# Three-pass projections and query-key products in f16 parts instead of float32r, in an encoder block

## The chip, the cores and the metric

One core of a Trainium2 chip runs the whole kernel. The metric is the time of an execution on the device in microseconds, as the median of several runs. A profile of one further execution comes with it. Engines are named as in the profile: PE does matmuls (PEld is its weight load), DVE, ACT and POOL work element by element on 128 partitions, and SP only issues DMAs here. Each engine runs its own instructions in order, and waits at an instruction whose input isn't there yet.

## The reference: what is computed

One layer of an encoder block on 1024 positions with 1024 features, in float32. Cut to what matters:

```python
h = x @ w_in                                   # (1024, 1024) @ (1024, 3328)
q_a, k_a, v_a, z_a, q_b, k_b, v_b, z_b = split(h)
# group a: 8 heads of 64; grid of 16 x 64 positions, window of 8 x 16 positions, bias per head
s = q_a . k_a * 64 ** -0.5 + rel_bias          # softmax over the 128 keys of the window
# group b: 8 query heads on 2 key heads, rotary positions, |i - j| <= 128, one sink logit per head
s = rotary(q_b) . rotary(k_b) * 64 ** -0.5     # softmax over the band and the sink
mixed = concat(y_a * silu(z_a), y_b * silu(z_b))
x = layer_norm(2 ** 0.25 * x + mixed @ w_out)
```

## The kernel before

**Split operands.** PE gets float32 accuracy from products of parts. An operand is split into a high part (a copy that rounds) and a low part (the rest), and each product is made of three matmuls: high with high, high with low, low with high. In this kernel the parts of x, of the input and output weights, of the queries and keys are float32r (32 bits wide); those of v and of the softmax weights are f16, with powers of two as scales, which for v are found on chip from its column maxima.

**First stage, v.** x arrives transposed in 16 tiles `xT[half, k]` of 128x512, k being one of 8 blocks of features and half one of two halves of the positions. `load_x` loads a tile into one of four `xr` buffers, ACT copies its high part, and DVE subtracts. v (640 columns) needs all of x: for the first half of the positions eight PSUM banks are filled side by side while x and the v weights arrive; then for the second half eight groups of 24 matmuls follow, one bank after the other. `v_out` (L369) copies a bank to SBUF on ACT and takes running maxima on DVE. This stage stands in a `manual_schedule` section (L377): every engine gets the instructions of that section in the order in which they are written. The rest up to the steps is ordered by the compiler.

**Projections.** The other 21 blocks of 128 columns of `w_in` are projected in the order `ORDER`: zb0, z0, zb1, kb, qb0, z1 ahead of the steps, and then 15 inside them. `project(name)` (L280) makes 2 halves x 8 k x 3 parts = 48 matmuls of 512 columns at L292. A weight block comes in two tiles m (256 KB each): `w_load` (L136) loads a tile, `w_split` (L142) makes the high part on ACT (L150) and the low part on POOL (L154). `evac` (L242) takes the result out of PSUM: a gate z by Silu or Tanh, a group-b query or key through `rope`, and queries and keys by `split_q` and `split_k` into stacks (`qs`, `ks`) that hold the high part on one half of the partitions and the low one on the other; POOL copies the key parts to the other half (L217).

**V scaling.** After zb0 the maxima of v are transposed on PE, turned into powers of two, and v is scaled, split, written to HBM and copied there into windows (`vd`, `vwin`), from which group a gathers.

**Steps.** There are 128 units, 64 of group b and then 64 of group a, one per step: 128 queries of one head against 256 to 384 keys. The section is again one of written order. In step i PE makes the two query-key matmuls of unit i (`stage_qk`, L533 and L534), DVE adds the bias and takes the minimum (L540), ACT does the exponential (L556). One step later `stage_tr` splits the weights in f16 (ACT L566, DVE L567) and SP transposes them by a DMA. Every four steps `stage_pv` (L595) multiplies four units with v, and every eight the outputs are transposed and multiplied with the gates. Between these `pump_to` puts projection matmuls, and at the end the first output matmuls, as a filling whose pace is given by `FILL_AT` (project number against step). `enq` puts splits and loads into queues per engine, from which each step takes one or two (`pop`). `stage_load` loads a bias tile four steps ahead (`LD`).

**Output.** `wo_split` splits 16 output weight tiles, eight of them in the steps at `WO_AT`, loaded at `WO_LD`; `m_queue` splits the gated outputs of group b at `M_AT`. `final` (L722) does the rest and the layer norm.

**Memory.** Pools of tiles with a fixed number of buffers: `big` (32 of 128x512 float32r) holds the parts of x and later those of the output weights; `wp` the weight tiles; `zp` the gates; `kq` the stacks, which are also used for gated outputs.

Of the kernel before, what the change touches and what calls it, by code (L numbers as in the profile page):

```python
# [23 lines left out]
PSCALE = 2.0 ** 14  # L24
LTT, LPP, BP, BH, BR, ND, NA, NX, F1 = 1, 5, 2, 7, 3, 1, 1, 6, 0.2
# [6 lines left out]
ZTAG = {"z3": "zv", "zb3": "zc", "z2": "zs"}  # L32
# [3 lines left out]
WO_TAG = ("wr", "wr", "wr", "wh", "wl", "wh", "wl", "wh", "wl")  # L36
# [12 lines left out]
def hybrid_block(ctx, tc, xT, x, wt, wv, wo, bias, sink, gain, lbias, cos, sin, bmask, out):  # L49
# [4 lines left out]
    big = ctx.enter_context(tc.tile_pool(name="big", bufs=32))  # L54
# [13 lines left out]
    def half_tile(name):  # L68
        return big.tile([128, 512], F32R, tag="big", name=name)

    xh, xl = {}, {}
    for half in range(2):
        for k in range(KT):
            xh[half, k] = half_tile(f"xh{half}{k}")
            xl[half, k] = half_tile(f"xl{half}{k}")
    zt = {}

    def zslot(name, tag="z"):
        return zp.tile([128, S], F32, tag=tag, name=name, bufs=5 if tag == "z" else 1)
# [6 lines left out]
    vsch = const.tile([128, 6], F32, name="vsch")  # L86
# [7 lines left out]
    def stk(kind):  # L94
        if kind == "q":
            return tiles["kq"].tile([128, S], F32R, tag="qs", name="qs", bufs=4)
        return tiles["kq"].tile([128, S], F32R, tag="ks", name="ks", bufs=8)
# [38 lines left out]
    def w_load(m):  # L136
        if m < NH:
            raw = wp.tile([128, 4, 128], F32, tag="wr", name=f"wr{m}", bufs=3)
            nc.sync.dma_start(raw, wt[m // 2, m % 2])
            raws[m] = raw  # L140

    def w_split(m):  # L142
# [16 lines left out]
        load_ops["w", m + 3] = enq("sp", lambda: w_load(m + 3), o)  # L159
# [3 lines left out]

    def split_q(p, half, src, dep=None):
        sl = slice(512 * half, 512 * half + 512)
        grid = not isinstance(p, str)
        ops = []

        def aps(j):
            if ("q", p, j) not in stks:  # L170
                stks["q", p, j] = stk("q")
            t = stks["q", p, j]
            a, o = slice(64 * j, 64 * j + 64), slice(64 - 64 * j, 128 - 64 * j)
            if grid:
                hi, lo = (t[r, sl].rearrange("p (b r c) -> p r b c", b=4, r=8) for r in (a, o))
                return hi, lo, src[a].rearrange("p (r b c) -> p r b c", b=4, r=8)
            return t[a, sl], t[o, sl], src[a]

        def hi(j):
            h, l, v = aps(j)  # L180
            nc.scalar.copy(h, v)

        def lo(j):
            h, l, v = aps(j)
            nc.vector.tensor_sub(l, v, h.bitcast(F32))

        prio = 0 if dep is None else 1
        for j in range(2):
            o = enq("act", lambda j=j: hi(j), dep, prio=prio)
            ops.append(enq("dve", lambda j=j: lo(j), o, prio=prio))  # L190
# [3 lines left out]
    def split_k(p, half, src, dep=None):  # L194
        sl = slice(512 * half, 512 * half + 512)
        ops, dup = [], []

        def aps(j):
            if ("kh", p, j) not in stks:
                stks["kh", p, j] = stk("kh")  # L200
                stks["kl", p, j] = stk("kl")
            return (stks["kh", p, j], stks["kl", p, j],
                    slice(64 * j, 64 * j + 64), slice(64 - 64 * j, 128 - 64 * j))

        def hi(j):
            h, l, a, o = aps(j)
            nc.scalar.activation(h[a, sl], src[a], AF.Copy, scale=0.125)  # L207

        def lo(j):
            h, l, a, o = aps(j)  # L210
            nc.vector.scalar_tensor_tensor(l[a, sl], src[a], 0.125, h[a, sl].bitcast(F32),
                                           op0=ALU.mult, op1=ALU.subtract)

        def dup_(j, w):
            h, l, a, o = aps(j)
            t = (h, l)[w]
            nc.gpsimd.tensor_copy(t[o, sl], t[a, sl])  # L217

        prio = 0 if dep is None else 1
        for j in range(2):  # L220
            o1 = enq("act", lambda j=j: hi(j), dep, prio=prio)
            o2 = enq("dve", lambda j=j: lo(j), o1, prio=prio)
            ops.append(o2)
            dup.append(enq("pool", lambda j=j: dup_(j, 0), o1))
            dup.append(enq("pool", lambda j=j: dup_(j, 1), o2))
# [3 lines left out]
    def rope(ps, half):  # L229
# [5 lines left out]
        o1 = enq("act", lambda: nc.scalar.copy(raw, ps), prio=0)  # L235
# [6 lines left out]
    def evac(name, half, ps):  # L242
# [17 lines left out]
        if name in ORDER[:3]:  # L260
            nc.scalar.activation(zt[e][:, sl], ps, AF.Silu)
            return []
        o = enq("act", lambda: nc.scalar.activation(zt[e][:, sl], ps, AF.Tanh, scale=0.5), prio=0)
# [5 lines left out]
    def z_col(e):  # L269
        c = e if e < 4 else 4 + (e - 4) // 2  # L270
        return (vsc if e in (4, 0, 5) else vsch)[:, c:c + 1]
# [8 lines left out]
    def project(name):  # L280
        n = ORDER.index(name)
        w_split(2 * n + 2)
        for half in range(2):
            ps = new_group()
            for k in range(KT):
# [5 lines left out]
                for i, (a, b) in enumerate(((h, xh), (h, xl), (l, xh))):  # L291
# [674 lines left out]
```

## Time and profile before

| | us |
|---|---|
| median of 3 runs (lowest, highest) | 483.23 (482.37, 483.33) |
| the profiled execution | 481.19 |
| its span, first to last instruction | 479.4 |
| v stage: first matmul of v to last | 3.8 to 61.9 |
| projections ahead of the steps | 61.8 to about 128 |
| steps | about 124 to 397 |
| output and layer norm | to 479.4 |

The granted clock of PE is 0.996 over the span. ACT is busy for 13.72 us of the 40 between 60 and 100, and POOL for 14.61. The longest groups of the page are the three of L292 with 336 matmuls each (133.9, 132.0 and 131.6 us); a matmul's listed length (393 to 398 ns) is from its start to its modelled end and overlaps the next one's, so that paces are read from the distances of starts, or from the merged pieces of the chain.

Durations that come up later: ACT cast of a weight tile 610 ns (L150), POOL subtraction of a weight tile 1324 ns (L154), DVE subtraction for x 690 ns (L333), DMA of a weight tile 3.1 us from issue to landing (median of 42), of a bias tile 3.7 (288 KB) and 4.6 (384 KB).

### The profile page before, as it was taken

To read this page: it belongs to the slowest core of one execution; us is meant where nothing else is said; L and a number is where in the kernel's file an instruction comes from. 1 tells how busy PE (TensorE), PEld (TensorE's weight loads), DVE (VectorE), ACT (ScalarE), POOL (GpSimd) and SP (SyncE) were. 2 spreads that over 40 slices of the span, in tenths; PEclk is the share of its full clock that TensorE was granted. 3 is DMA by queue.
4 is the path that set the end of the run, shared out by engine and by line. 5 is a ranking of instruction groups with operands and counts; after the bars stand their busy time and mean duration, and the time that the engine had idled before them with its cause. 6 is when DMAs were issued, how large, how long until landed. Compare 5 with 4: busy or idle time off the path is not lost.

```text
span 479.4 us, 9121 instructions
## 1 busy us (share of the span) xinstructions
PE 466.5 (97%) x3240; PEld 400.6 (84%) x3240; DVE 325.2 (68%) x772; ACT 255.2 (53%) x601; POOL 165.5 (35%) x153
## 2 busy tenths in 40 slices
PE   8999999999999999999999999999999999999993
PEld 6999988888788888888888888888888778788883
DVE  5726505868567968888787767767767739379644
ACT  5651122352577858777777676766768737012101
POOL 0030012597236246464124225122535317125521
PEclk9999999999999999999999999999999999999998
DMA  7862001477276666567889898999999979216211
GB/s 252 260 210 86 1 0 45 132 244 243 60 110 105 163 111 128 100 143 117 176 138 222 199 189 198 229 207 212 209 190 203 208 194 398 110 42 193 97 45 64
DMA packets 132381, 74.73 MB, mean 156 GB/s; under 512 B 101104, under 2 KB 117488, under 8 KB 132080
## 3 DMA queue, kind: packets, MB, share of 16 engines
q1 hardware_dynamic: 132192, 74.00, 66.3%
q8 instruction: 25, 0.41, 0.4%
q14 instruction: 20, 0.16, 0.1%
q10 hardware_dynamic: 144, 0.15, 0.1%
HBM read 43.72 MB, written 9.96 MB: 112 GB/s over the span
## 4 chain that ended last, share of the span: by engine, by line
PE 84%; DVE 7%; DMA 3%; ACT 3%; issue 2%; SPq 0%; ACTq 0%; DVEq 0%
PE ps_pj L292 42%; PE ps_t L595 6%; PE ps_s L705 6%; PE ps_pj L705 4%; PE ps_s L362 4%; PE ps_s L533 4%; PE ps_s L534 4%; PE ps_t L705 3%; PE ps_pj L362 3%; PE ps_t L362 3%; DMA tr<-split 2%; PE ps_ot L705 2%; PE ps_ot L362 1%; PE ps_ot L615 1%; DMA xraw<-in_xT 1%
## 5 line engine op out<-in xcount | busy, mean ns | idle before, releaser
L292 PE MATMUL ps_pj<-xh,wh 128*128 128x512 f32 x336 | 133.9, 398 | 0.8 <-ACT rp_raw L235 0.5
L292 PE MATMUL ps_pj<-xl,wh 128*128 128x512 f32 x336 | 132.0, 393 | 0.0
L292 PE MATMUL ps_pj<-xh,wl 128*128 128x512 f32 x336 | 131.6, 392 | 0.0
L154 POOL TENSOR_TENSOR wl<-wr,wh 128x512 fp32r<-128x512 f32 x42 | 55.5, 1324 | 169.5 <-ACT wh L150 119.4
L556 ACT ACTIVATE ps_s<-sn,nm 128x385 f32<-128x385 f32 (+3 forms) x128 | 70.5, 551 | 52.7 <-DVE nm L540 51.3
L567 DVE SCALAR_TENSOR_TENSOR split<-ps_s,split 128x384 f16<-128x384 f32 (+2 forms) x128 | 65.6, 513 | 20.4 <-ACT split L566 19.7
L292 PEld LDWEIGHTS ps_pj<-xh,wl 128*128 128x128 f32 x336 | 63.1, 188 | 12.9
L292 PEld LDWEIGHTS ps_pj<-xh,wh 128*128 128x128 f32 x336 | 63.2, 188 | 10.9 <-DVE z L264 0.7
L292 PEld LDWEIGHTS ps_pj<-xl,wh 128*128 128x128 f32 x336 | 63.2, 188 | 9.4
L566 ACT ACTIVATE split<-ps_s 128x384 f16<-128x384 f32 (+2 forms) x128 | 58.0, 453 | 11.6 <-DMA tr<-split 9.7
L540 DVE CUSTOM_DVE_ANT_0 sn<-ps_s,bm,nsk 128x384 f32<-128x384 f32 (+1 forms) x64 | 37.2, 582 | 19.0 <-PE ps_s L534 18.2
L540 DVE CUSTOM_DVE_ANT_0 sn<-ps_s,bias 128x288 f32<-128x288 f32 (+1 forms) x64 | 32.3, 505 | 20.9 <-PE ps_s L534 19.1
L533 PE MATMUL ps_s<-ks,qs 128*128 128x384 f32 (+2 forms) x128 | 41.3, 322 | 0.1
L534 PE MATMUL ps_s<-ks,qs 128*128 128x384 f32 (+2 forms) x128 | 41.1, 321 | 0.0
L217 POOL CAST ks<-ks 64x512 fp32r<-64x512 f32 x40 | 27.2, 679 | 35.8 <-ACT ks L207 19.4
L595 PEld LDWEIGHTS <-tr 128*128 128x128 f16 (+1 forms) x1104 | 35.6, 98 | 4.0 <-DMA tr<-split 1.7
L150 ACT CAST wh<-wr 128x512 fp32r<-128x512 f32 x42 | 25.6, 610 | 10.2 <-PE ps_pj L292 8.5
L762 ACT ACTIVATE sd<-mv,eps 128x1 f32<-128x1 f32 x8 | 2.4, 295 | 52.5 <-DVE mv L760 52.5
L533 PEld LDWEIGHTS ps_s<-ks,qs 128*128 128x128 f32 x128 | 24.0, 188 | 7.0 <-DVE split L567 1.8
L534 PEld LDWEIGHTS ps_s<-ks,qs 128*128 128x128 f32 x128 | 24.0, 188 | 5.0
L556 ACT ACTIVATION_READ_ACCUMULATOR ps_s<-sn,nm 128x1 f32 x128 | 24.1, 188 | 0.0
L671 POOL TENSOR_TENSOR wol<-wor,woh 128x512 fp32r<-128x512 f32 x11 | 15.6, 1430 | 22.8 <-ACT woh L667 19.8
(191 smaller groups left out, 871.2 us busy)
## 6 DMA issues: line engine op xcount, KB each, us to landing
wr<-in_wt SPq DMA_DIRECT2D x42, 256.0 KB, 3.1
bias<-in_bias SPq DMA_DIRECT2D x16, 288.0 KB, 3.7
wor<-in_wo SPq DMA_DIRECT2D x16, 256.0 KB, 5.3
xr<-in_x SPq DMA_DIRECT2D x8, 512.0 KB, 8.0
xraw<-in_xT SPq DMA_DIRECT2D x15, 256.0 KB, 4.5
out<-xr SPq DMA_DIRECT2D x14, 256.0 KB, 2.0
bias<-in_bias SPq DMA_DIRECT2D x8, 384.0 KB, 4.6
wvraw<-in_wv SPq DMA_DIRECT2D x7, 320.0 KB, 4.0
```

What stands on the lines that cost most here:

```text
L154: nc.gpsimd.tensor_sub(l, raws.pop(m), h.bitcast(F32))
L217: nc.gpsimd.tensor_copy(t[o, sl], t[a, sl])
L292: nc.tensor.matmul(ps, a[:, k % 4, :], b[half, k], start=(k == 0 and i == 0), stop=(k == KT - 1 and i == 2))
L362: nc.tensor.matmul(ps[:, :320], lh[t // 4, k][:, ts], rh[k][:, cs], start=(k == 0 and i == 0), stop=(k == KT - 1 and i == 2))
L533: nc.tensor.matmul(ps[:, :n], q, sl[0], start=True, stop=False)
L534: nc.tensor.matmul(ps[:, :n], q, sl[1], start=False, stop=True)
L540: nc.vector.tensor_tensor_reduce(sn[:, :n], ps[:, :n], bias_t, -1.0, init, op0=ALU.add, op1=ALU.min, accum_out=nm)
L556: nc.scalar.activation(pt[:, :m], sn[:, :m], AF.Exp, bias=nm, scale=-1.0, accum_out=sm[:, k:k + 1])
L566: nc.scalar.activation(hl[:, :m, 0, :c], src, AF.Copy, scale=PSCALE)
L567: nc.vector.scalar_tensor_tensor(hl[:, :m, 1, :c], src, PSCALE, hl[:, :m, 0, :c], op0=ALU.mult, op1=ALU.subtract)
L595: nc.tensor.matmul(ps[:, HD * m:HD * m + HD], a, b_, start=(i == 0), stop=(i == len(mms) - 1))
L705: nc.tensor.matmul(ps, lh[:, ts], rh[:, cs], start=(e == EO[0] and i == 0), stop=(e == EO[-1] and i == 2))
```

## The change

Projections of q, k and z and the query-key products use f16 parts in place of float32r parts; v and the output product keep float32r. To keep the parts in range, each operand is scaled by a power of two that the kernel finds itself: one for x (`sc[:, 0]`), one for the first four weight blocks, which are `NG0` (`sc[:, 1]`), and one for the other 17 (`sc[:, 2]`).

- x keeps its float32r parts for v. Its largest absolute value per partition is taken by 16 DVE reductions (`x_max`), `chain(0)` makes the scale of it with one PE transpose; then x is loaded a second time and split in f16 (`x16_part`: high on ACT; low on DVE, or in two operations on POOL for k = 1, 3, 5).
- The weights are loaded once more for a bound of their size (`scan_load`, `scan`: ACT Abs with a running sum, 42 tiles): eight within the v stage and 34 after it; `chain(1)` and `chain(2)` make the scales. `w_split` gets a scale on ACT and a second POOL operation, a multiplication in place.
- Scales are taken out again where results leave PSUM: `inv` for the gates, `QSCALE` for queries and keys, `sg` in the operation at L540 (a pointer in place of -1.0), and `rsg`, by which POOL multiplies each bias tile.
- The queries of group a are put in window order by the projection's moving operand and not by the split.
- The running maxima of v are taken three banks at a time, behind the parts of x.
- Output weights 0 to 3 are loaded at steps 60 to 74 and split at 67 to 79 (before: loaded at 111 to 115, split at 115 to 122); `M_AT` goes from 115 to 118 for one split. Tiles get other buffers: `big` is 16 of twice the size, the stacks are f16 and closed ahead of `final`, gated outputs lie in `big` and in `final`'s own pool.

```diff
+QSCALE = 2.0 ** -23
+NG0 = 4
-M_AT = [105, 112, 115, 120]
-WO_AT = [115, 116, 117, 122, 132, 132, 133, 133]
-WO_LD = [111, 112, 113, 115, 129, 129, 130, 130, 131, 132, 132, 133, 133]
+M_AT = [105, 112, 118, 120]
+WO_AT = [67, 71, 75, 79, 132, 132, 133, 133]
+WO_LD = [60, 61, 70, 74, 129, 129, 130, 130, 131, 132, 132, 133, 133]
...
         def hi():
-            h = wp.tile([128, 4, 128], F32R, tag="wh", name=f"wh{m}")
-            l = wp.tile([128, 4, 128], F32R, tag="wl", name=f"wl{m}")
+            h = wp.tile([128, 4, 128], F16, tag="wh", name=f"wh{m}")
+            l = wp.tile([128, 4, 128], F16, tag="wl", name=f"wl{m}")
             parts[m] = (h, l)
-            nc.scalar.copy(h, raws[m])
+            nc.scalar.activation(h, raws[m], AF.Copy, scale=scale)

         def lo():
             h, l = parts[m]
-            nc.gpsimd.tensor_sub(l, raws.pop(m), h.bitcast(F32))
+            raw = raws.pop(m)
+            nc.gpsimd.tensor_scalar(raw, raw, scale, 1.0, op0=ALU.mult, op1=ALU.mult)
+            nc.gpsimd.tensor_sub(l, raw, h)
+
+        g = 1 if m < 2 * NG0 else 2
+        scale = sc[:, g:g + 1]
...
-                for i, (a, b) in enumerate(((h, xh), (h, xl), (l, xh))):
-                    nc.tensor.matmul(ps, a[:, k % 4, :], b[half, k],
+                for i, (a, b) in enumerate(((h, x16h), (h, x16l), (l, x16h))):
+                    mv = b[half, k]
+                    if name[0] == "q" and name[1] != "b":
+                        mv = mv.rearrange("p (r b c) -> p b r c", b=4, r=8)
+                    nc.tensor.matmul(ps, a[:, k % 4, :], mv,
...
+        def scan_load(m):
+            scans[m] = vp.tile([128, 512], F32, tag="xr", name="wscan", bufs=4)
+            nc.sync.dma_start(scans[m], wt[m // 2, m % 2].rearrange("p k c -> p (k c)"))
+
+        def scan(m):
+            g = 0 if m < 2 * NG0 else 1
+            i, t = m - 2 * NG0 * g, scans.pop(m)
+            nc.scalar.activation(t, t, AF.Abs, accum_out=wm[g][:, i:i + 1])
+
+        def chain(i, src, tag):
+            g = gm[:, i:i + 1]
+            nc.vector.tensor_reduce(g, src, axis=AXX, op=ALU.max)
+            ps = bank(tag)
+            nc.tensor.transpose(ps[:, :128], g.to_broadcast([128, 128]), identf)
+            nc.vector.tensor_reduce(g, ps[:, :128], axis=AXX, op=ALU.max)
...
+        def x16_part(j):
+            half, k = x2[j]
+            raw = x2raw.pop(j)
...
+            nc.scalar.activation(h, raw, AF.Copy, scale=sc[:, 0:1])
+            if k in (1, 3, 5):
+                nc.gpsimd.tensor_scalar(raw, raw, sc[:, 0:1], 1.0, op0=ALU.mult, op1=ALU.mult)
+                nc.gpsimd.tensor_sub(l, raw, h)
+            else:
+                nc.vector.scalar_tensor_tensor(l, raw, sc[:, 0:1], h, op0=ALU.mult, op1=ALU.subtract)
...
             for i in range(8):
                 v_out(banks[i], i // 2, i % 2)
+            for k in range(4, KT):
+                x_max(0, k)
+            for k in range(KT):
+                x_max(1, k)
             for i in range(8):
                 ps = bank(tags[i])
                 for k in range(KT):
                     v_mms(ps, 4 + i // 2, i % 2, k)
                 v_out(ps, 4 + i // 2, i % 2)
+                if i < 2:
+                    for m in range(4 * i, 4 * i + 4):
+                        scan(m)
+                        if i == 0:
+                            scan_load(m + 4)
+                        else:
+                            x2_load(m - 4)
+                if i == 1:
+                    chain(0, xm, "ot")
+                if 2 <= i < 6:
+                    for j in range(4 * (i - 2), 4 * (i - 2) + 4):
+                        x16_part(j)
+                        x2_load(j + 4)
+                if i == 2:
+                    for m in range(4):
+                        w_load(m)
+                if i == 3:
+                    chain(1, wm[0], "ot")
+                if i == 4:
+                    w_split(0)
+                    w_split(1)
+                if i == 5:
+                    for nm, src, tag in (("cos", cos, "zc"), ("sin", sin, "zs")):
+                        tiles[nm] = zslot(nm, tag)
+                        nc.sync.dma_start(tiles[nm], src)
+                    nc.vector.tensor_scalar_mul(nsk, sk, -1.0)
+                if i > 1:
+                    v_max(3)
...
+        for m in range(2 * NG0, 2 * NG0 + 4):
+            scan_load(m)
         pump_all(["zb0"])
+        for m in range(2 * NG0, NH):
+            scan(m)
+            if m + 4 < NH:
+                scan_load(m + 4)
...
-                st["bias"] = bt
+                bv = bt[:, :, :n]
+                op = enq("pool", lambda: nc.gpsimd.tensor_scalar(bv, bv, rsg, -1.0, op0=ALU.mult, op1=ALU.mult),
+                         prio=0)
+                st["bias"] = bt, op
...
-        nc.vector.tensor_tensor_reduce(sn[:, :n], ps[:, :n], bias_t, -1.0, init,
+        c = 0 if g == "b" else 1
+        nc.vector.tensor_tensor_reduce(sn[:, :n], ps[:, :n], bias_t, sg[:, c:c + 1], init,
                                        op0=ALU.add, op1=ALU.min, accum_out=nm)
...
-    pump_all(ORDER[1:NPRO])
+    pump_all(ORDER[1:NG0 - 1])
+    chain(2, wm[1], "ot")
...
+    pump_all(ORDER[NG0 - 1:NPRO])
```

More of the change, by code (lines that the diff above doesn't have):

```diff
@@ L234, in rope @@
         sw = tiles["ap"].tile([128, 512], F32, tag="va", name="rp_sw", bufs=5)
-        o1 = enq("act", lambda: nc.scalar.copy(raw, ps), prio=0)
+        o1 = enq("act", lambda: nc.scalar.activation(raw, ps, AF.Copy, scale=QSCALE), prio=0)
         o2 = enq("dve", lambda: nc.vector.stream_shuffle(sw, raw, SWAP), o1)
@@ L640, in hybrid_block, with m_alloc @@
     EO = (4, 5, 6, 7, 0, 1, 2, 3)
-    def m_alloc(e, pair):
-        mh[e], ml[e] = (stk(pair) for _ in range(2))
+    def m_alloc(e, pool):
+        tag, bufs = ("big", 16) if pool is big else ("m", 8)
+        mh[e], ml[e] = (pool.tile([128, S], F32R, tag=tag, name=f"m{e}", bufs=bufs) for _ in range(2))
     def m_split(e, sl, hi, lo):
```

195 lines of the change are left out of this document (116 added, 79 removed).

## The prediction

> **What bounds the kernel now.** I read the page's engine table first, then the 40 slices, the chain that ended last, and then stretches of the chain in order of time.
>
> ```profile
> PE 466.5 (97%) x3240; PEld 400.6 (84%) x3240; DVE 325.2 (68%) x772; ACT 255.2 (53%) x601; POOL 165.5 (35%) x153
> ...
> PE   8999999999999999999999999999999999999993
> ```
>
> PE works in every slice but the last, and the chain gives it 84% of the span. A busy PE isn't yet a fast one, so the next question is the distance from one matmul to the next. Three pieces of the chain, about step 32, show it:
>
> ```profile
> 187.29 1.39 PE ps_pj L292 x6
> 188.68 0.12 PE ps_s L533
> 188.80 0.11 PE ps_s L534
> ...
> 190.51 0.98 PE ps_t L595 x33
> ```
>
> Six projection matmuls of 512 columns take 1.39 us, so one costs 0.231 us; in zb0 (61.95 to 72.86, 48 of them) it is 0.227. 33 f16 matmuls of 64 columns, each with its own weights, take 0.98, or 0.0295 each. The rows of weight loads say that the two kinds load at different rates, and PE's timeline that the kernel begins with six f16 matmuls of 512 columns (start, length, then the group):
>
> ```profile
> L292 PEld LDWEIGHTS ps_pj<-xl,wh 128*128 128x128 f32 x336 | 63.2, 188 | 9.4
> ...
> L595 PEld LDWEIGHTS <-tr 128*128 128x128 f16 x816 | 26.7, 98 | 3.0 <-DMA tr<-split 1.4 <-issue 1.3
> ```
>
> ```profile
> 1.19 2.74 PE L322 MATMUL ps_ot<-warm 128*128 128x512 f16 x6 [1.19 <-DVE warm L319]
> ```
>
> DVE is the next engine: 95.6 of the 120 us from 130 to 250, ACT 87.7.
>
> **The gain on PE.** Columns stream at one rate whatever the type (projection, 512 columns, 0.227; v, 320 columns, 7.04 us for 48 or 0.1467: 0.0803 for 192 columns, or 0.418 ns a column), so a float32r matmul is 512 x 0.418 = 0.214 and 0.013 to 0.017 more. An f16 matmul of 64 columns is 0.0268 and 0.0027 more. No row has an f16 matmul of 512 columns at full clock: the six of the start stand 0.438 apart (1.19 to 3.82), twice the 0.219 that is wanted, on a clock that I take to be half. Bounds: 0.214, and 0.231 as now; I take 0.217, since the f16 row with real weights is nearest.
> - Prologue, six projections: 288 x (0.227 - 0.217) = 2.9 us, and some 0.3 of stalls: 3.2.
> - Steps, fifteen projections: 720 x (0.231 - 0.217) = 10.1. After each PV block the first float32r matmul stands 0.31 before the next one (191.33 to 191.64); with f16 weights that is 0.217, for some 30 blocks 2.4 more beyond what is counted.
> - Query-key, 256 matmuls: those of 384 columns are 0.175 (0.35 a pair, 1.74 us between two steps' fills less 1.39), for f16 0.163: 160 x 0.012 = 1.9; the 96 smaller at 0.008, 0.8.
> - Off it: between 350 and 410 PE has 57.65 of 60 us, and waits there for transposes (3.7 to 4.1 us each in the chain); what PE gains there it waits, so I take off 1.3. And L540 gets a pointer in place of an immediate. Today its b form, with one pointer operand, takes 616 ns, the a form without 555 (both 384 columns), so up to 0.06 us for each of 128 units. DVE would be at about 99 of 112 us in the stretch after 130. Bounds 0 to 7.7 (all of it on the path); I take 1.5.
>
> The steps so give 15.2 - 2.8 = 12.4 us, the prologue 3.2.
>
> **What is added ahead of zb0.** The diff puts into the second half of v (33.8 to 61.8, eight groups of 24 matmuls, 3.52 us each) a maximum of x, eight weight scans, a second load of x and its f16 split. That section keeps its written order on each engine: DVE sat idle for sk although v was copied long before.
>
> ```profile
> 39.83 0.17 DVE L402 TENSOR_SCALAR nsk<-sk 128x8 f32<-128x8 f32 x1 [9.91 <-DMA sk<-in_sink]
> 39.91 0.48 DVE L372 SCALAR_TENSOR_TENSOR vmax<-v,vmax 128x320 f32<-128x320 f32 x1
> ```
>
> So I follow the order. ACT comes to scan 0 behind the copy of group 0, at 37.8. A scan is a 128x512 cast (0.61), an accumulator read (0.19) and a little: 0.85 (0.82, a 128x512 ACTIVATE with two pointers, L796, and the read would be 1.0). Scans 0 to 3 end at 41.3, each frees an xr buffer, the loads land 2.6 us later (72.00 to 74.60 for one wr load alone; 3.1 is the median), scans 4 to 7 end at 45.2. Each frees a buffer for the second x: the first is there at 45.3, and the scale of x (three reductions, a transpose, five small DVE operations at 0.17) by 42.2. A part then costs ACT 0.70 (0.61 and a pointer) and DVE 0.69, or, for k = 1, 3, 5, POOL two operations. The subtraction is a 1.30 row. The multiplication has no like row: a 64x512 cast 0.68, the only TENSOR_SCALAR 1.075 for 256 columns, so 0.7 to 2.15; I take 1.3, as for the TENSOR_TENSOR of this width.
>
> GpSimd is the place for a rule: the Trainium skill ("GPSIMD Engine Reference", section 4.1) says that it is about half as fast as VectorE for operations with two inputs and roughly at line rate with one. By its section 3.1 one input of 512 columns would be some 0.77 us (an estimate), a pair 2.1 and not 2.6, and the stall below 7.7 and not 8.8; the 1.075 row for 256 columns speaks against it, and I stay with 2.6.
>
> Part 1 leaves POOL at 49.7, part 3 at 52.3. The SP queue is written in order, so load 7 goes out at 52.4 and lands at 55.0; ACT 55.7, DVE 56.5. Only behind this does DVE reach the reduction for the first range of the weights, and its transpose lies **on PE between groups 3 and 4**. PE ends group 3 at 48.0 and waits to 56.8: 8.8 us. Bounds: 7.6 (multiplication 0.7, twice), 10.5 (2.15, and 1.8 more in zb0), and 1.2 on top with loads of 3.1. From there groups 4 to 7 cover the rest: the last x part is ready near 75.6 and zb0 wants it at 79. Without that cover zb0 itself would wait nearly as long, since x isn't split before 71. With the transpose and its wait zb0 starts at 70.9, not 61.8: 9.1.
>
> A stall that long also costs clock:
>
> ```profile
> 470.00:479.40 9.40, 1.31 (x12) 1.10 (x10) 4.19 (x9) 1.44 (x3) 1.67 (x2) 0.80 0.15 56
> ```
>
> After PE's last matmul at 471.3 the mean grant is 0.80; a fall to half gives that if it comes 4.3 us after PE stops. At the start PE needed from 1.2 to about 4.7 for the full pace. 3.5 us at half is 1.75 lost, once. (0 if the grant holds.)
>
> The twelve maxima and the later vmax fill a DVE that had 9.9 us free; bm, sk, cos and sin wait for nothing. They cost nothing unless DVE runs past 79, where zb0 still has its own cover.
>
> **The second range.** The 34 other scans (256 KB each, on SP like the rest) reuse the four buffers, from 67.6 to 75.6 on. A turn is 2.6 + 0.85 + 0.1 for four: 0.89 each, 30 us; ACT has 29 us of scans and 13.7 of other work (its busy time from 60 to 100). So they end between 108 and 118; with 1.7 for the chain and 0.7 for ACT's part, qb0, the first that needs it, has weights between 111 and 121. PE comes to qb0 at 72.7 + 4 x 10.4 = 114.3, and its third matmul wants POOL's part, 2.6 later. I take 2.5 us (0 to 9).
>
> **In the steps** POOL gets 30 multiplications (39 us by the value above) and 24 bias scalings of 576 or 768 columns (1.4 to 1.9 by 1.3 for 512; 38 us), on 130 us busy of 355. Each bias scaling also holds POOL's queue until the load lands (3.7 to 4.6): behind it lie the weight subtractions, wanted eight steps later, and key copies; the scaled bias is wanted four steps, some 8 us, later. I cost it at nothing; one late turn in three would be 8 x 2 = 16 us, but POOL's lag shortens the wait that it follows. The four early output splits take 2.5 of ACT and 4.3 of POOL away from steps 115 to 122, where nothing waits for them; their loads go onto SP at steps 60 to 74, 0.4 us of issue each, between transposes that SP issues every 2 us. Key and query splits keep their counts and widths.
>
> **Sum.** 9.1 + 1.75 + 2.5 - 3.2 - 12.4 = -2.25, and some 0.6 that the four early output splits may save where ACT is at 8.1 of 10 (340 to 350): -3. The profiled run took 481.19 around a span of 479.4; its median beside others is 483.23, 2.0 higher. 478.2 in a like run, **480.2** as a median.
>
> **Rivals.**
> - *The prologue hides better* (0.24). Multiplication at 0.7, scans done by 108, DVE never late: 7.9 + 1.75 - 3.2 - 15.2 - 0.6 = -9.4: 474. For it: DMA lies idle from 40 to 70, 0.0 of 10 us. Against: the order on PE is written down.
> - *The second range comes late* (0.17, slower). Same place, PE ahead of qb0, one mechanism: the scan loads fall behind the copies of v into its windows. A weight load behind these took 12.3 us and not 2.6. 9.7 later: 490. It decides from 3 us on. For: both move to about 110. Against: the scans stand first in the program.
> - *DVE becomes the bound in the steps* (0.11, slower). It is at 8.8 of 10 from 210 to 220; pointer operands and a faster PE bring it past 9. Half the step gain lost, 6.2: 486.5.
> - *f16 streams no faster at 512 columns* (0.05, slower): no gain at all, 9.1 + 1.75 + 2.5 - 0.6 = +12.8: 496.
> - The change does what it says: the types are in the diff.
>
> **Numbers.** The forecast has 0.43, with 475 to 486 of its own. A run of this kernel tells about 0.2%, 1 us, from none. Faster: the hidden prologue 0.24 and 0.29 of the forecast. Slower: the three rivals, 0.33, and 0.06 of the forecast. Same: 0.08. The range, 471 to 492, leaves out the last rival, the ends of the late range and the best of the hidden one.
>
> **What would show it.** Projection matmuls 0.217 apart. A PE gap ahead of v's fifth group of 24, ended by DVE, near 8.8 us, and slow matmuls behind it; zb0 from about 72.7. A small gap before qb0. Steps with DVE near 9 of 10 and no PE gap. I am wrong in sign if the two gaps together pass 14 us, or if PE waits for DVE or a scaled bias in the steps.

## The result and the profile after

| | before | changed |
|---|---|---|
| median of 4 runs (lowest, highest) | 482.80 (481.50, 483.33) | 537.27 (534.91, 539.32) |
| span of the profiled execution | 479.4 | 533.7 |
| zb0's first matmul | 61.8 | 75.2 |
| qb1's first matmul (seventh projection) | 129.8 | 161.2 |
| projections 7 to 14 (group b's half of the steps) | 128.3 | 124.9 |
| projections 15 to 21 (group a's half) | 114.8 | 142.5 |
| from the last projection to the end | 106.5 | 105.1 |

The change costs 54 us: the ratio is 1.113 [1.107, 1.120]. 31 of them arise ahead of the steps and 28 in the second half of the steps; the first half and the output give 5 back. From the page of the changed kernel, the lines that answer to those shown of before, and the chain's shares:

```profile
PE 466.1 (87%) x3243; PEld 302.3 (57%) x3243; DVE 359.5 (67%) x823; ACT 296.5 (56%) x701; POOL 220.9 (41%) x231
...
PE   8997697796599999899997839599788999999994
...
PEclk9999699989699999999999987799799999999998
...
PE 60%; DMA 11%; issue 8%; DVE 7%; ACT 7%; POOL 6%; SPq 1%; POOLq 0%; ACTq 0%; DVEq 0%
```

PE works as long as before (466 us), though its matmuls are shorter, since some of them ran at half clock (below), and it has 55 us more of idle time: in slices 4 to 11 and 22 to 31, counted from 1, and around PE's holes the granted clock falls. The groups on the page (before the bar busy us and mean ns of one, behind it idle time and what ended it) name who ended the waits:

```profile
L296 PE MATMUL ps_pj<-xf,wl 128*128 128x512 f16 x336 | 130.2, 389 | 29.1 <-POOL wl L163 29.1
L296 PEld LDWEIGHTS <-wh 128*128 128x128 f16 x672 | 64.8, 99 | 73.5 <-issue 9.3
...
L162 POOL TENSOR_SCALAR wr<-wr,sc 128x512 f32<-128x512 f32 x42 | 34.1, 812 | 67.6 <-ACT wh L157 50.6
...
L614 POOL TENSOR_SCALAR bias<-bias,rsg 128x576 f32<-128x576 f32 (+1 forms) x24 | 19.2, 798 | 90.6 <-DMA bias<-in_bias 63.0
```

PE waited 29.1 us for low parts of weights, which POOL makes. In the profile of before the matmuls with a low part of a weight had no wait:

```profile
L292 PE MATMUL ps_pj<-xh,wl 128*128 128x512 f32 x336 | 131.6, 392 | 0.0
```

POOL is busy for 41% only. It waits itself, 63 us for bias loads (L614), and whatever is behind it in its queue waits too. The matmuls themselves are as forecast: a weight load is 99 ns (188 before), and the starts of the 1008 projection matmuls stand 0.216 us apart in the median.

### The profile page after: what moved, and what is told of

Read it like the earlier page. It is cut to its first block, busy times and chain, and to the rows that moved or that the text cites. A ratio compares the mean times of both kernels' runs of the same rounds, so it can differ in the third digit from the quotient of the medians.

```text
span 533.7 us, 9570 instructions
## 1 busy us (share of the span) xinstructions
PE 466.1 (87%) x3243; PEld 302.3 (57%) x3243; DVE 359.5 (67%) x823; ACT 296.5 (56%) x701; POOL 220.9 (41%) x231
## 4 chain that ended last, share of the span: by engine, by line
PE 60%; DMA 11%; issue 8%; DVE 7%; ACT 7%; POOL 6%; SPq 1%; POOLq 0%; ACTq 0%; DVEq 0%
PE ps_pj L296 25%; PE ps_s L828 6%; PE ps_t L702 5%; PE ps_t L828 4%; PE ps_pj L828 4%; DMA wscan<-in_wt 4%; DMA bias<-in_bias 3%; PE ps_pj L366 3%; ACT wscan L388 3%; POOL wl L163 3%; PE ps_s L639 3%; PE ps_t L366 3%; PE ps_s L640 2%; PE ps_ot L828 2%; PE ps_s L366 2%
## 5 line engine op out<-in xcount | busy, mean ns | idle before, releaser
L296 PE MATMUL ps_pj<-xf,wh 128*128 128x512 f16 x672 | 207.3, 388 | 8.9 <-ACT wh L157 5.5
L296 PE MATMUL ps_pj<-xf,wl 128*128 128x512 f16 x336 | 130.2, 389 | 29.1 <-POOL wl L163 29.1
L296 PEld LDWEIGHTS <-wh 128*128 128x128 f16 x672 | 64.8, 99 | 73.5 <-issue 9.3
L663 ACT ACTIVATE ps_s<-sn,nm 128x385 f32<-128x385 f32 (+3 forms) x128 | 70.3, 549 | 63.9 <-DVE nm L647 62.8
L296 PEld LDWEIGHTS <-wl 128*128 128x128 f16 x336 | 33.5, 100 | 72.5 <-POOL wl L163 34.2
L162 POOL TENSOR_SCALAR wr<-wr,sc 128x512 f32<-128x512 f32 x42 | 34.1, 812 | 67.6 <-ACT wh L157 50.6
L647 DVE CUSTOM_DVE_ANT_0 sn<-ps_s,bias,sg 128x288 f32<-128x288 f32 (+1 forms) x64 | 36.1, 565 | 37.5 <-PE ps_s L640 30.2
L614 POOL TENSOR_SCALAR bias<-bias,rsg 128x576 f32<-128x576 f32 (+1 forms) x24 | 19.2, 798 | 90.6 <-DMA bias<-in_bias 63.0
L163 POOL TENSOR_TENSOR wl<-wr,wh 128x512 f16<-128x512 f32 x42 | 49.7, 1185 | 3.2
L647 DVE CUSTOM_DVE_ANT_0 sn<-ps_s,bm,nsk 128x384 f32<-128x384 f32 (+1 forms) x64 | 40.8, 638 | 8.9 <-PE ps_s L640 8.3
L639 PE MATMUL ps_s<-ks,qs 128*128 128x384 f16 (+2 forms) x128 | 40.2, 314 | 6.0 <-DVE split L674 4.7
L640 PE MATMUL ps_s<-ks,qs 128*128 128x384 f16 (+2 forms) x128 | 40.2, 314 | 0.0
L157 ACT ACTIVATE wh<-wr,sc 128x512 f16<-128x512 f32 x42 | 29.4, 709 | 11.9 <-PE ps_pj L296 11.9
L828 PE MATMUL ps_s<-wo,m 128*128 128x512 f32 (+1 forms) x144 | 32.5, 374 | 0.0
```

Of the source, the lines that this page charges most:

```text
L163: nc.gpsimd.tensor_sub(l, raw, h)
L296: nc.tensor.matmul(ps, a[:, k % 4, :], mv, start=(k == 0 and i == 0), stop=(k == KT - 1 and i == 2))
L639: nc.tensor.matmul(ps[:, :n], q, sl[0], start=True, stop=False)
L640: nc.tensor.matmul(ps[:, :n], q, sl[1], start=False, stop=True)
L647: nc.vector.tensor_tensor_reduce(sn[:, :n], ps[:, :n], bias_t, sg[:, c:c + 1], init, op0=ALU.add, op1=ALU.min, accum_out=nm)
L663: nc.scalar.activation(pt[:, :m], sn[:, :m], AF.Exp, bias=nm, scale=-1.0, accum_out=sm[:, k:k + 1])
```

## The experiments

Times are medians. The expectations count projections from 0, so that group a's half is 14 to 20; it begins with q1, and not with k2 as the text of e2 has it. A wait of PE is given as the profile's idle time; the expectations give some of them up to 0.2 us longer. All runs are shown against runs of the kernel before on the same chip (481.7 to 482.2).

### Bias scaling on POOL: e2, e4, e12

e2 takes it away: group a's queries and keys get their true size where they are split, and L647 gets -1.0 again.

```diff
-                op = enq("pool", lambda: nc.gpsimd.tensor_scalar(bv, bv, rsg, -1.0, op0=ALU.mult, op1=ALU.mult),
-                         prio=0)
...
-                              src[a], dep is None)
+                              src[a], kinv[a, :] if dep is None else None)
```

> Group a's queries and keys are brought to true size in their splits, so POOL scales no bias tile and the softmax operation of group a has its immediate again; all else as in the changed kernel. Theory: the bias scaling stands on POOL's queue until its load lands, the weight subtractions lie behind it, and SP's next weight load (with the transposes behind it) waits for these; the second half of the projections in the steps costs 28 us more than before (k2 to the last projection matmul 142.5 against 114.8). Then 503 to 511, and no PE wait over 1.5 us is ended by POOL in the steps. Rival: POOL's multiplication of each weight tile and the pointer operands are the price. Then 529 or more, with the waits for POOL's weight subtraction still there.

512.82 (508.36 to 515.54): 24.5 us less than the changed kernel, and group a's half takes 116.9 instead of 142.5. The time is 1.8 above the theory's range, and far from the rival's: one slow projection is left (q2, 22.6 us), in which PE waits 2.4 us for a cast of ACT and 1.5 for a low part. e4 keeps the operation and only queues it three steps behind its load, so that POOL doesn't stand at it while the load is under way.

```diff
                 op = enq("pool", lambda: nc.gpsimd.tensor_scalar(bv, bv, rsg, -1.0, op0=ALU.mult, op1=ALU.mult),
-                         prio=0)
+                         Later(), prio=0)
```

> The changed kernel with each bias scaling put into POOL's queue three steps after its load, and not in the same step; the work is the same. If POOL's waiting for the load is the cost in the second half of the steps: 505 to 515. If it is POOL's work: 530 or more. If the scaled bias then comes too late for DVE, the time lies between, with DVE waiting for POOL at the softmax operation.

515.32 (513.43 to 516.12), 22 less and 0.3 above the range for the waiting, with the same 19.2 us of POOL work; the 2.5 us to e2 lie within the spread of the runs. So it is mainly not the work that costs, it is the place in the queue. How it passes on can be read in the timelines of the changed kernel's POOL, SP and PE (start, length, work, and in brackets the idle time before it and what ended it):

```profile
308.32 2.49 POOL L794 TENSOR_TENSOR wo<-wor,wo 128x512 fp32r<-128x512 f32 x2
318.54 0.74 POOL L614 TENSOR_SCALAR bias<-bias,rsg 128x576 f32<-128x576 f32 x1 [7.73 <-DMA bias<-in_bias]
319.26 0.69 POOL L162 TENSOR_SCALAR wr<-wr,sc 128x512 f32<-128x512 f32 x1
320.03 1.15 POOL L163 TENSOR_TENSOR wl<-wr,wh 128x512 f16<-128x512 f32 x1
```

```profile
302.06 1.21 SPq L677 DMA_TRANSPOSE tr<-split  x1
308.39 0.33 SPq L146 DMA_DIRECT2D wr<-in_wt  x1
308.82 2.87 SPq L677 DMA_TRANSPOSE tr<-split  x1
...
315.05 0.57 SPq L612 DMA_DIRECT2D bias<-in_bias  x1
```

```profile
321.24 0.61 PE L296 MATMUL ps_pj<-xf,wl 128*128 128x512 f16 x1 [4.89 <-POOL wl L163]
```

It is a ring. SP stands from 303.3 to 308.39 at a weight load whose buffer POOL frees with its subtraction (307.21 to 308.36). Behind that load lie the transposes and the next bias load, which so goes out at 315.05 only. POOL reaches that bias at 310.8, waits 7.7 us for it, and the subtraction that PE needs stands behind. The lag of one engine becomes the lag of the other. Over group a's half SP's waits for POOL's low parts add up as follows (us in total, times, longest), where the kernel before has none:

```profile
SPq L146 <- POOL wl L163: 20.4, 7, 5.0
```

e12 puts this one part into the kernel before, alone, with a factor of 1:

```diff
+                op = enq("pool", lambda: nc.gpsimd.tensor_scalar(bv, bv, one, 1.0, op0=ALU.mult, op1=ALU.mult),
+                         prio=0)
+                st["bias"] = bt, op
...
+            need(op)
```

> The kernel before with one part of the change alone: POOL multiplies each bias tile, by 1, in the operation and at the place of the changed kernel. Theory (POOL waits at the head of its queue for a bias load; weight subtractions stand behind it, and SP waits for POOL before the next weight load, with transposes behind): 12 to 25 us slower, 494 to 507, and projections 14 to 20 take 127 or more instead of 114.8. Rival (it needs POOL's doubled weight work beside it): less than 5 us slower.

496.47 (494.82 to 498.92), ratio 1.029 [1.024, 1.035]: 14.2 us, and group a's half 129.3. The same ring with nothing else of the change (SP waits 16.4 us for POOL's low parts here, and DVE 7.3 us for the scaled bias), from its groups, SP, POOL and PE:

```profile
L514 POOL TENSOR_SCALAR bias<-bias,one 128x576 f32<-128x576 f32 (+1 forms) x24 | 19.3, 803 | 88.8 <-DMA bias<-in_bias 71.9
```

```profile
322.08 1.21 SPq L576 DMA_TRANSPOSE tr<-split  x1
327.36 0.34 SPq L141 DMA_DIRECT2D wr<-in_wt  x1
```

```profile
326.05 1.29 POOL L156 TENSOR_TENSOR wl<-wr,wh 128x512 fp32r<-128x512 f32 x1
333.08 0.91 POOL L514 TENSOR_SCALAR bias<-bias,one 128x768 f32<-128x768 f32 x1 [5.75 <-DMA bias<-in_bias]
333.95 1.27 POOL L156 TENSOR_TENSOR wl<-wr,wh 128x512 fp32r<-128x512 f32 x1
```

```profile
335.28 0.50 PE L294 MATMUL ps_pj<-xh,wl 128*128 128x512 f32 x1 [2.21 <-POOL wl L156]
```

### Scans, search and multiplications: e1, e3, e5

e1 sets the scales by memset (x 2^12, weights 2^11); scans, maxima of x and the three searches are left out, the second load of x and the multiplications stay.

```diff
+        for i, e in enumerate((12, 11, 11)):
+            nc.vector.memset(rs[:, i:i + 1], 2.0 ** -e)
+            nc.vector.memset(sc[:, i:i + 1], 2.0 ** e)
...
-                        scan(m)
-                    chain(0, xm, "ot")
-                    chain(1, wm[0], "ot")
-    chain(2, wm[1], "ot")
```

> The scales are constants set at the start: the 42 scans of the weights, the 16 maxima of x and the three chains are left out; x is still loaded and split a second time, and the bias tiles are still scaled. Theory: the search for the scales is what holds PE ahead of the steps (qb1 starts 31 us later than before: 161.2 against 129.8). Then 537 - 31 to 537 - 25: 506 to 512, and qb1 starts within 6 us of 130. Rival: the second load of x and its split, with a second POOL operation for each weight tile, are the price. Then at most 12 us come back: 525 or more, and zb0 still starts beyond 70.

525.98 (520.81 to 527.09): 11.3 less. That is the rival's number, but not the late start of zb0 that it named: zb0 starts at 63.9 and is slow itself (a wait of 5.3 us for wl, then half clock), and qb1 starts at 151.2 against 129.8. So most of the prologue's loss is not the search. e3 is e1 and e2 together.

> Both of the former: constant scales, no scaling of bias tiles. If the two costs are separate they add: 537 - 28 - 28 = 481, between 473 and 487. If the f16 pace is worth its full 19 us once nothing waits: 464 to 472. If a third cost is left in the steps (DVE, the second POOL operation): above 487.

499.84 (496.65 to 502.85): 37.4 less than the changed kernel, where 11.3 + 24.5 is 35.8; the two add up. But they come to far less than the 56 that was expected, and the time is the one for a third cost. e5 goes on from e3 and leaves the weights unscaled.

```diff
-            nc.gpsimd.tensor_scalar(raw, raw, scale, 1.0, op0=ALU.mult, op1=ALU.mult)
             nc.gpsimd.tensor_sub(l, raw, h)
```

> The kernel with fixed scales and without the bias scaling, and in addition the parts of the q, k and z weights are left unscaled, so that POOL makes a low part in one subtraction, as before. Left out: the scans, the search for scales, the scaling of the weights. Theory (in the prologue PE waits for POOL's second operation and for what stands between the two): the waits for wl of 5.4 us in zb0 and 4.4 us in z1 fall to under 3 and under 1, the half clock behind them goes, qb1 starts at 143 or earlier (149.6 without this edit), and the time is 490 to 494. Rival (the prologue's loss is the second load of x and DVE's and ACT's work on it; the multiplication lies beside it): qb1 starts at 147 or later, and the time is 497 to 500.

490.91 (487.16 to 492.22), 8.9 less, qb1 from 140.0. The wait for wl in z1 is gone, that in zb0 is 3.2 and not under 3. So the second operation on POOL lay on the path ahead of the steps; from qb1 to the last projection the time only goes from 241.7 to 239.2. Why it did can be read in POOL's timeline of the changed kernel, which the compiler ordered there, with PE's line below:

```profile
130.92 2.82 POOL L162 TENSOR_SCALAR wr<-wr,sc 128x512 f32<-128x512 f32 x2
133.80 0.94 POOL L220 COPY ks<-ks 64x512 f16<-64x512 f16 x1
134.84 0.69 POOL L162 TENSOR_SCALAR wr<-wr,sc 128x512 f32<-128x512 f32 x1
135.60 2.63 POOL L220 COPY ks<-ks 64x512 f16<-64x512 f16 x3
138.31 1.15 POOL L163 TENSOR_TENSOR wl<-wr,wh 128x512 f16<-128x512 f32 x1
```

```profile
139.52 0.61 PE L296 MATMUL ps_pj<-xf,wl 128*128 128x512 f16 x1 [8.11 <-POOL wl L163]
```

A pair split by others is what PE waits for: three tiles are multiplied and four key copies made before the first subtraction.

### The early output splits: e6, e9

e6 is e3 with the four splits at the steps of before; e9 is e5 with the same edit.

```diff
-WO_AT = [67, 71, 75, 79, 132, 132, 133, 133]
-WO_LD = [60, 61, 70, 74, 129, 129, 130, 130, 131, 132, 132, 133, 133]
+WO_AT = [115, 116, 117, 122, 132, 132, 133, 133]
+WO_LD = [111, 112, 113, 115, 129, 129, 130, 130, 131, 132, 132, 133, 133]
```

> The kernel with fixed scales and without the bias scaling, with output weights 0 to 3 loaded and split at the steps of before (111 to 122 instead of 60 to 79). Theory (the one slow projection that is left in the steps, the 16th from 307.0 to 328.8, is slow because an output split takes ACT's turn from a weight's cast, and its load takes SP's time): that projection takes 16 to 17 us, the time is 493 to 496. Rival (the turns are short in any case in group a's steps, and late splits take them later): the slow projection stays or another one of the last five takes its place, 498 to 502.

492.03 (490.13 to 495.08), 7.8 less than e3; the slow projection takes 15.6 us instead of 21.8. In e3 ACT, which gets one queued operation per step, made an output split and two key casts ahead of the weight's cast that PE waited 2.8 us for.

> The kernel with fixed scales, without bias scaling and with unscaled weight parts, and with output weights 0 to 3 split late: of the change only the f16 products, the second load and split of x, and the buffers are left. It leaves out all the scans and the search. Theory (the late splits are worth the same 7.8 us as in the kernel with the multiplications): 482 to 485, and the 17 to 20 us that it still lies above the kernel before in f16 are those of the prologue (second load of x, v in float32r). Rival (with POOL freed the slow projection is gone anyway): 488 to 491.

484.37 (481.15 to 487.93), 6.5 less than e5, as the theory had it; against the kernel before the ratio is 1.003 [1.000, 1.006].

### The prologue's order: e7, e10, e11

e7 makes the low parts of weight tiles 0 to 13 in one operation on DVE.

```diff
+            if m < 2 * NPRO + 2:
+                nc.vector.scalar_tensor_tensor(l, raw, scale, h, op0=ALU.mult, op1=ALU.subtract)
+                return
```

> The changed kernel with one edit: the low parts of weight tiles 0 to 13, those ahead of the steps, in one operation on DVE, as the changed kernel does for most of x, in place of two on POOL. Theory (the order of POOL's pairs in the prologue makes PE wait): the wait of 8.3 us at 131 and the half clock behind it go, the start of qb1 comes from 161.2 to 150 or earlier, and the time is 523 to 528. Rival (the wait moves: DVE, with the maxima of v and rope in the same stretch, makes the low parts as late): qb1 at 157 or later, 533 or more.

531.02 (530.27 to 532.48) and qb1 from 155.2: neither theory. The wait of 8.1 us is gone; in its place PE waits 5.8 us at 101.3 for ACT's Silu and 2.6 and 1.9 us at 127 and 131 for a cast and a low part. e10 puts the search of the first scale behind v's group 6.

```diff
-                if i == 3:
-                    chain(1, wm[0], "ot")
-                if i == 4:
+                if i == 6:
+                    chain(1, wm[0], "pj")
```

> The changed kernel with one edit: the scale of the first weights (the transpose that PE waited 8.7 us for) is made behind v's group 6 instead of group 3, and the first two weight tiles are split there. Theory (that wait is paid in full): zb0 starts at 64 to 67 instead of 75.2, and the time is 526 to 531. Rival (what comes behind waits as long: the scale of the other weights hangs on ACT's 34 scans, which set the start of qb0 at 130 in any case): qb0 at 127 or later and 534 to 538.

538.26 (535.33 to 542.74): the rival's number, and qb0 at 129.5, but zb0 starts later, not earlier. From PE's timeline and DVE's:

```profile
74.97 0.45 PE L394 MATMUL ps_pj<-identf,gm 128*128 128x128 f32 x1 [15.40 <-DVE gm L392]
```

```profile
74.67 0.15 DVE L392 TENSOR_REDUCE gm<-wm 128x1 f32<-128x8 f32 x1
```

The reduction moved behind more maxima of v and parts of x on DVE than PE moved behind groups of v. zb0 came 5.9 us later and qb0 1 us earlier: the two waits don't add up, since the scans of the second range ended at 114.4 and not at 124.1. e11 is e2, e6's edit, e7 and e10 together, all scales found on chip.

> The changed kernel with all scales still found on chip, and four edits together: no bias scaling on POOL (queries and keys of group a are brought to true size where they are split), output weights 0 to 3 split late, low parts of weight tiles 0 to 13 on DVE, and the scale of the first weights behind group 6. Theory (the costs are separate and add up: 24.5 + 7.8 + 6.3 + 0 to 9): 490 to 499. Rival (the costs overlap in one prologue that ACT's scans set): 500 to 506. Neither has it below the 482 of the kernel before.

500.41 (499.16 to 502.97), at the lower edge of the rival's range. Yet the edits nearly add up: 36.9 us come back, and one by one they were worth 24.5, 7.8 and 6.3, less 1.0 for e10's, in all 37.6. Its steps are faster than before's (234.2 from qb1 to the last projection, 243.1 before); qb1 starts at 156.6, and that is the loss that remains.

### What f16 is worth: e8, e13, e14

e8 is the kernel before with f16 tiles for the parts of x, of the input weights and of the stacks, without scales.

```diff
-            h = wp.tile([128, 4, 128], F32R, tag="wh", name=f"wh{m}")
-            l = wp.tile([128, 4, 128], F32R, tag="wl", name=f"wl{m}")
+            h = wp.tile([128, 4, 128], F16, tag="wh", name=f"wh{m}")
+            l = wp.tile([128, 4, 128], F16, tag="wl", name=f"wl{m}")
```

> The kernel before with the parts of x, of all input weights (v's too) and of the stacks as f16 tiles, with no scales at all; every instruction of the other engines in the order of before. It leaves out the scaling, on which f16's range depends. Theory (f16's shorter matmuls come through where nothing else is added): the prologue gains 3.2, the steps 12 to 15, v 384 x (0.147 - 0.135) = 4.6, in all 458 to 463. Rival (in the steps other engines, or the DMA transposes, set the pace, so that only a part of PE's gain is seen, as in the first eight projections of the steps of the changed kernel, which gained 3.4 where 7 was expected): 467 to 473.

465.39 (464.41 to 467.69), ratio 0.965 [0.960, 0.970]: faster than both kernels. 16.8 us, between the theories; 4.5 of it come from v, which the change left in float32r. The two halves of the steps (start, end, length, busy us of PE, PEld, DVE, ACT, POOL, the clock, the DMA engines' share, GB/s), before and then e8:

```profile
129.80:258.10 128.30, 128.29 (x1035) 110.65 (x1036) 102.09 (x284) 94.19 (x243) 53.23 (x47) 1.00 0.70 134
258.10:372.90 114.80, 114.13 (x977) 97.90 (x977) 82.49 (x232) 80.92 (x212) 38.68 (x41) 1.00 1.06 206
```

```profile
122.90:243.90 121.00, 120.15 (x1035) 67.67 (x1035) 100.89 (x280) 92.70 (x240) 50.04 (x45) 1.00 0.77 140
243.90:358.00 114.10, 109.07 (x979) 62.26 (x977) 82.84 (x236) 80.58 (x214) 37.51 (x42) 0.99 1.11 209
```

The first half gains 7.3, the second 0.7: PE has 5 us of idle time there, and the packets' time on the 16 DMA engines is 1.11 of the stretch (0.77 in the first half; 1.06 before). So a second limit seems to lie just below PE's there. ACT shows whom it holds; its waits for transposes add up to 14.6 us in this half, and to 6.0 before:

```profile
309.52 0.41 ACT L566 ACTIVATE split<-ps_s 128x288 f16<-128x288 f32 x1 [2.73 <-DMA tr<-split]
```

e13 loads three bias tiles and uses them for all; e14 loads all, from ACT's queue.

```diff
+                if ("bt", b) not in st:
...
-                nc.sync.dma_start(bt[:, :, :n], bias
+                nc.scalar.dma_start(bt[:, :, :n], bias
```

> The kernel before in f16 (465.4), in which three of the 24 bias tiles of group a are loaded and used for all; 21 loads of 288 or 384 KB are left out. It leaves out the right bias for all heads but the first. Theory (in group a's steps the DMA engines or SP set the pace, not PE): projections 14 to 20 take 106 to 109 us instead of 114.1, and the time is 457 to 460. Rival (they are PE's, and the 7 us are lost in single waits that have nothing to do with transfers): 113 or more, and 464 to 466.

458.98 (458.38 to 459.38): group a's half takes 107.1, the seven us that were missing.

```profile
244.70:351.80 107.10, 106.12 (x977) 61.55 (x976) 81.93 (x232) 80.31 (x212) 37.40 (x42) 1.00 0.82 164
```

> The kernel before in f16 (465.4), with the 24 bias loads issued by ACT instead of SP; nothing is left out. If SP's issuing sets the pace (21 issues of 0.57 us, in all 13.6 with their waits): projections 14 to 20 take 106 to 110 and the time is 458 to 462. If the DMA engines do: 113 to 115, and 464 to 467.

461.33 (459.87 to 463.16): the time that was expected if SP's issuing sets the pace, but group a's half, 111.6 in the profiled run (463.16, the slowest of the six), lies between the two. Six of the seven projections run at full pace (PE busy for 90.50 of 90.5 us), the last takes 21.1 us with waits of 1.7 and 1.1 for transposes.

```profile
245.30:335.80 90.50, 90.50 (x836) 52.51 (x834) 69.18 (x193) 66.72 (x176) 28.55 (x35) 1.00 1.08 217
335.80:356.90 21.10, 17.29 (x148) 9.73 (x145) 13.35 (x39) 15.16 (x40) 9.35 (x8) 0.94 1.04 210
```

So SP's issuing is one limit: its issues in the trace of e8 take 102 of the 114 us, and with the bias loads on ACT's queue ACT's waits for transposes fall from 14.6 to 4.7 us (1.7 in e13). A share of 1.08 by itself doesn't hold PE, as the first of these two lines shows. Whether the transfers cost anything beside the issuing isn't told apart: e13 leaves out both. e14 is the fastest kernel with all of the reference's loads; like e8 it has no guard for f16's range.

### The account

Along one order of undoing, each step a difference of two medians: bias scaling 24.5 (to e2), scans and search 13.0 (to e3), weight multiplications 8.9 (to e5), early splits 6.5 (to e9), and 19.0 from e9 to e8, nearly all ahead of qb1 (141.8 against 122.9). There e9 has the second load and split of x, its POOL work, v in float32r, and other buffers. In all 71.9, against 16.8 that f16 gives: 55. What of the last 19.0 belongs to which part wasn't tried.

## Why the prediction was wrong

**What held.** f16 matmuls of 512 columns at 0.217 (0.216 measured), of 384 at 0.163 (0.162). The stall of PE ahead of v's fifth group, forecast at 8.8:

```profile
58.21 0.47 PE L394 MATMUL ps_ot<-identf,gm 128*128 128x128 f32 x1 [8.58 <-DVE gm L392]
```

The chain was the one that was reckoned (POOL's pair, the next load of x, ACT's cast, DVE's part, the reduction). The size is in part luck: the wait ended at 58.2 and not at 56.8, but group 3 ended late as well, at 49.6 and not at 48.0. And on the way two prices were off and made up for each other. POOL's multiplication, 1.3 in the sum, is 0.69 where POOL is alone (the mean of L162's 42 is 0.81), and DVE's maxima took more:

```profile
51.89 1.43 DVE L441 SCALAR_TENSOR_TENSOR vmax<-v,vmax 128x320 f32<-128x320 f32 x1
...
53.77 0.48 DVE L441 SCALAR_TENSOR_TENSOR vmax<-v,vmax 128x320 f32<-128x320 f32 x1
```

The same operation takes 1.43 while POOL subtracts (51.71 to 52.97), and 0.48 when POOL is idle. The 1.075 row misled. The estimate of 0.77 for one input, worked out from the Trainium skill ("GPSIMD Engine Reference", section 3.1), was the nearer one. The Trainium skill ("GPSIMD Engine Reference", section 1) also says that POOL and DVE contend for SBUF when a DVE instruction has two SBUF inputs; the two lines agree, though no run here changed that alone.

**The step that failed: "I cost it at nothing"** for POOL in the steps, with the reason that "POOL's lag shortens the wait that it follows". It cost 24.5 us within the change and 14.2 alone (e12). The other price in the same paragraph, "one late turn in three would be 8 x 2 = 16 us", was of the right size. The wait isn't shortened, because the bias load isn't independent of POOL: SP sends it behind a weight load that waits for POOL. I had named what stands behind POOL, and not what stands behind SP's wait for POOL. In the steps the multiplications did lie nearly beside the rest (2.5 us by e5); what they cost, they cost ahead of the steps. And "some 0.6" that the early splits may save were 6.5 to 7.8 lost: the steps they were moved to were as full on ACT (8.2 of 10 us from 295 to 305 in e3) as those they left (8.1 of 10, as the prediction has it).

**The second range, 2.5 (0 to 9).** Place and mechanism were right, the size wasn't: qb0 starts at 130.4, behind a wait of 2.1 us for a cast, and its first matmul with a low part at 139.5. Three terms were short. A turn of scans: the chain shows loads of 3.7 and 5.7 us where I had 2.6, so that the last scan ended at 124.1 and not by 118:

```profile
77.90 3.66 DMA wscan<-in_wt
...
83.52 5.74 DMA wscan<-in_wt
```

The search behind it took 5.3 us (124.18 to 129.5) and not 1.7, since rope of kb and a key split stand between its operations on DVE. And POOL's part took 8.1 where 2.6 was reckoned, by the order shown above. All in all qb1 came 31.4 us later, for 9.1 + 1.75 + 2.5 - 3.2 = 10.2: zb0 13.4 later, 10.5 more from zb0 to qb0, and 7.5 from qb0 to qb1. Between zb0 and qb0, where the prediction had no cost ahead of qb0's own wait, PE also waits for Silu (3.4 us), for another cast (1.5) and for a low part (1.9), and runs at half clock for 3.4 us.

**Cold clock "1.75, once".** It happened six times ahead of the output. Behind the first stall:

```profile
58.20:64.20 6.00, 5.99 (x23) 5.99 (x24) 3.82 (x13) 0.00 (x0) 0.00 (x0) 0.50 0.58 183
```

Six us of work at half rate are 3.0 lost. In all six, 28.1 us of PE work ran at 0.50: 14 us. These are within the parts of the account, not beside them. The lengths at half clock (3.4, 6.8, 10.2) are multiples of one window. The Trainium skill ("TensorE: Matmul & The Clock Gate", Part 1) says that the clock falls to half after an idle window of some 3.4 us and returns after a busy one; the trace agrees with the lengths, but not with an idle time of that length: half clock also came with a wait of 2.7 us (from 376.8), and in e8 with one of 2.0 (from 319.9), while a wait of 2.2 (from 87.3) had none. So a wait's length alone doesn't give its price in clock.

**The steps, 12.4.** e8 gives 8.0, of which 7.3 in group b's half. The prediction counted every matmul of group a's half as time won but for 1.3 us, though the page of before had the transposes in the chain; e13 shows that the 7 us are there once the transfers are fewer. In the changed kernel even group b's half gained 3.4 only. PE's query-key matmuls wait 3.0 us for DVE there and 0.7 in e8, and the operation at L647, now with a pointer, takes 672 ns where it took 616 (384 columns): the 0.06 that was reckoned. No run changed the pointer alone.

**Rivals.** None gave the time. "The second range comes late" had the place but 9.7 us, and not the mechanism: the copies of v into the windows went out from 126.7 on, behind the last scan. DVE did not become the bound. What would prove the sign wrong was named: the two gaps were 8.6 and 8.1, together 16.7 us where 14 were the limit, and in the steps PE waited for low parts that stood behind a scaled bias.

## What to carry to other kernels

Before a DMA-dependent operation is put at the head of an in-order queue, follow the ring: who frees the buffers that the issuing queue waits for, and what lies behind that wait. A two-operation product on an engine that a compiler orders isn't a pair; price the waits between its halves, or make it one operation. And before counting a faster matmul as time, ask which limit lies next: here the queue that issues the transposes and loads, just below PE in half of the steps.

## What was not expected of the hardware

DVE's operation on two SBUF inputs took 0.48 us alone and 1.43 beside POOL's subtraction, but 0.48 beside POOL's TENSOR_SCALAR (at 50.67 in the changed kernel's trace), which then took 1.45 itself (at 50.18; 0.69 alone). f16 weights load in 99 ns where float32r take 188, but the starts of matmuls of 512 columns came only 15 ns closer.
